# FFN token operands made between the first products, and an attention merge that advances three times per attention step

## The chip, the cores and the metric

The kernel runs on one core of one Trainium2 chip. The metric is the device time of one execution in microseconds (us); of several runs the median is taken.

## What is computed

Two layers of an encoder over 1024 tokens with 1024 channels. Each layer has three residual steps. The change touches the end of the first and the beginning of the second.

```
h = rms_norm(x);  z = h @ w_in
merged = concat(rms_norm(o_attn), rms_norm(o_gm), rms_norm(o_conv))   # windowed attention, spatial gating, conv
x = x + merged @ w_out                                                # the mixer
hf = rms_norm(x, norm_ffn_g) @ w_gate_up                              # 1024 x 5632
x = x + (silu(hf[:, :2816]) * hf[:, 2816:]) @ w_down                  # the FFN
x = x + (p @ w_ple_proj) * sigmoid(rms_norm(x) @ w_ple_gate)
```

## The kernel before

**Layout and products.** Channels lie on the 128 partitions, tokens along the free axis, in two halves of 512 tokens. Every product of fp32 numbers is made of three fp32r matmuls (`step_mm`, L220 to L229): high part by high part, high by low, low by high. The high part is a rounded copy (`copy_h`, L122, on ACT), the low part is the rest (`sub_l` L125, `scaled_l` L128, on DVE). `load_w` (L205 to L217) loads 512 KB of weights from the SP queue into one of 3 buffers `raw`, makes the high part `wh` (L122 on ACT, or L215 on the engine handed in) and the low part `wl` (L216, on DVE or POOL); `wh` and `wl` have 3 buffers each. 38 tiles of 128 x 1024 (`U`) serve nearly everything else. The PSUM banks are three `pa` (`BA`), four `pt` (`BT`) and one `po`.

**Order of the work.** Each engine executes its instructions in one fixed order. It comes from the order of the code, which a scheduler of the framework then moves within limits at build time, and from generators that the code advances by hand: `bg.tick()` is called within products and advances the background generators by their rates. The attention is one such generator, `att_gen` (L963). One of its steps, t, handles one block of 128 tokens of one group of heads in five parts that end in `yield`; after the eighth block of a half of the tokens it starts that half's `merge_attn` (L924), which multiplies by the softmax denominators (L942, L943), squares and sums over channels (L944 on ACT, L946 on POOL, L950 on PE), takes the power -0.5 (L270, POOL), spreads it over the partitions (L281, PE) and writes the operands `mhl` (L957, L122, L128). A merge has 10 parts, and `att_gen` advances it once per step (L1034), at the end of the step.

**Mixer's end.** `wo_first` multiplies the parts of `w_out` that need no attention. `bg.until(att, ...)` (L1255) then runs the attention until half 0 is merged. `wo_second(0)` (L1085) adds the attention part for half 0, takes the sum into X (L1100, DVE), makes the FFN operands `hl` of that half (`norm_add`) and the norm's factor per token, `nrm[0].bc` (`norm_stat` L292 and L270, `norm_bcast` L281 and L298; the tile is named `st`).

**FFN.** The gate and up products are made by a scheme with seven products in place of eight for each pair of 128 output columns, over two halves of the tokens and two of the channels. `first(j)` (L1119) makes the products of half 0 for pair j: 48 matmuls into four banks, which DVE takes out (L1138, L1140, L1141, L1145), and writes two partial results to memory from the ACT queue. `token_forms(k)` (L1160), for k = 0 to 3, makes the other token operands `tf`: four rows of X times gain and norm (`normed`, L1157, DVE), differences of them (L1167, L1169 on DVE, L1168, L1172 on POOL) and five splits into high and low (L122 ACT, L125 DVE). `load_rest(j)` (L1179) loads the pair's weights into four tiles `rw` and one `sm`, and `rest(j)` (L1191) forms sums of weights on POOL (L1228 to L1231), splits them (L122, L125) and makes 120 matmuls on `tf`. There are 11 pairs. The order is first(0) to first(3), the rest of the attention, first(4), `wo_second(1)`, the four `token_forms`, first(5) to first(7) (`BEHIND` = 3), and then rest(0), first(8), rest(1), first(9), rest(2), first(10), rest(3) to rest(10). While `ahead` is true (first(0) to first(4)) the weights' high parts are made on DVE and the low parts on POOL, and `first` uses the three `pa` banks alone; later it uses all seven.

Of the kernel before, what the change touches and what calls it, by code (L numbers as in the profile page):

```python
# [43 lines left out]
PLE_LAG = 2  # L44
NP2 = NF // 2
AHEAD = 4
BEHIND = 3

C1 = 1
C2 = 2.0  # L50
# [21 lines left out]
def tile_encoder_trunk(ctx: ExitStack, tc: tile.TileContext, x, p, positions, norm_mix_g, w_in,  # L72
# [389 lines left out]
    for layer in range(DEPTH):  # L462
# [461 lines left out]
        def merge_attn(hb):  # L924
# [27 lines left out]
            r = small(4, "ar")  # L952
            rsqrt_cols(r, ps[:, 0:4], 1.0 / 512)
            yield
            ps = bcast_rows(r)
            for kt, o in enumerate(os):
                nc.vector.tensor_tensor(out=o, in0=o, in1=ps, op=ALU.mult)  # L957
# [5 lines left out]
        def att_gen():  # L963
# [4 lines left out]

            def at(i):
                return items[i] if 0 <= i < n else None  # L970

            def aside():
                while side:
                    if next(side[0], bg) is bg:
                        side.pop(0)
                    else:
                        break

            yield from q_split(0, 0)
            for t in range(n + 3):  # L980
                while zqs[at(t + 1).kv if at(t + 1) else 0] is None:
                    yield
                x, y, z, w = at(t), at(t - 1), at(t - 2), at(t - 3)
                nx = at(t + 1)
                if nx and nx.b % 2 == 0:
                    side.insert(0, q_split(nx.kv, nx.b // 2))
                if x:
                    x.begin()
                if y:
                    y.peak()  # L990
                    y.exp(0)
                if x:
                    x.score(0)
                yield
                if w:
                    w.value(2)
                    w.out()
                    if (t - 3) % 8 == 7:
                        merging.append(merge_attn((t - 3) // 8))
                aside()  # L1000
                yield
                if y:
                    y.exp(1)
                if z:
                    z.turn(0)
                if x:
                    x.score(1)
                aside()
                yield
                if y:  # L1010
                    y.exp(2)
                if z:
                    z.turn(1)
                if x:
                    x.score(2)
                yield
                if z:
                    z.value(0)
                if y:
                    y.exp(3)  # L1020
                aside()
                yield
                if z:
                    z.turn(2)
                if x:
                    x.score(3)
                if z:
                    z.value(1)
                aside()
                yield  # L1030
                if nx and nx.b % 2 == 0:
                    while (nx.kv, nx.b // 2) not in qts:
                        aside()
                for g_ in list(merging):  # L1034
                    if next(g_, bg) is bg:
                        merging.remove(g_)
            for g_ in merging:
                yield from g_

# [79 lines left out]
        def first(j):  # L1119
# [1 line left out]
            hl0, bc = nrm[0].hl, nrm[0].bc  # L1121
            c0 = 2 * j * P
            ws = [load_w(rows_of(w_gate_up[layer], 0, NK, off + c0, P), (NK, P),
                         nc.gpsimd if ahead else None, nc.vector if ahead else None)
                  for off in (0, DFF)]
            a, sm = T("sg"), U("sm")
            for i, (wh, wl) in enumerate(ws):
# [31 lines left out]

        def token_forms(k):  # L1160

            for hf in range(2):
                for m in (k, k + HK):
                    normed(hf, m)
            b11, b21, b12, b22 = X[0][k], X[0][k + HK], X[1][k], X[1][k + HK]
            t1 = T("t1")
            nc.vector.tensor_tensor(out=t1, in0=b12, in1=b11, op=ALU.subtract)  # L1167
# [93 lines left out]
        first(AHEAD)  # L1261
        wo_second(1)
        ahead = False
        for k in range(HK):
            token_forms(k)
        for j in range(AHEAD + 1, AHEAD + 1 + BEHIND):
            first(j)
        for j in range(NP2):
            load_rest(j)
            rest(j)  # L1270
# [151 lines left out]
```

## Time and profile before

| what | value |
|---|---|
| runs | 2505.62, 2507.15 and 2503.2 us; median 2505.62 us |
| the profiled execution | 2507.3 us, its span 2505.5 us |
| TensorE (PE) busy | 2327.1 us, 93% of the span |
| VectorE (DVE) busy | 1493.4 us, 60% |
| ScalarE (ACT) busy | 915.8 us, 37% |
| GpSimd (POOL) busy | 730.1 us, 29% |
| mean granted TensorE clock | 0.967 of full speed |

The two layers do the same work: a place at t us in layer 0 is found again some 1235 us later in layer 1. In layer 0 the attention ends and `wo_second(0)` starts at about 365 us, `wo_second(1)` runs from 474.6 to 496.4 us, and rest(0) starts at 556 us. In the rows, "idle before" is the time in which an engine stood still before an instruction, and "<-" names what ended it. Bracketed numbers in a timeline are the same for one instruction.

### The profile page before, as it was taken

How to read it: one execution, taken by the hardware profiler on the slowest of the kernel's cores; microseconds unless marked ns; L12 is line 12 of the kernel's file. 1: busy time of each engine (PE TensorE's matmuls, PEld its weight loads, DVE VectorE, ACT ScalarE, POOL GpSimd, SP SyncE). 2: the span in 40 equal slices, each digit the busy share in tenths (PEclk: the TensorE clock that was granted, in tenths of full speed). 3: DMA queues.
4: the chain of work that ended last, by engine and by line, in shares of the span. 5: the costliest groups of instructions: out<-in, count | busy, mean ns of one | idle time of the engine just before them, and what ended most of it. 6: DMA issues, size and time to landing. Idle time of an engine off the chain costs nothing. (4 is left out here: it accounts for less than half of the span.)

```text
span 2505.5 us, 30172 instructions
## 1 busy us (share of the span) xinstructions
PE 2327.1 (93%) x11404; PEld 1950.1 (78%) x11404; DVE 1493.4 (60%) x2307; ACT 915.8 (37%) x1610; POOL 730.1 (29%) x529
## 2 busy tenths in 40 slices
PE   7997977969999999999999898879689999999999
PEld 6996766847788888888789876768577888888887
DVE  7996676475665553626469666755856555526252
ACT  4346572132232243424323455612322222425242
POOL 4122415541344300104321233255424342001031
PEclk9998998989999999999999999989899999999999
DMA  6110513632543245543321123135345341736332
GB/s 200 44 55 9 177 34 97 214 110 93 190 163 110 94 161 174 176 135 106 100 68 39 35 76 110 58 119 181 101 160 173 118 146 52 234 123 210 100 91 70
DMA packets 237010, 294.78 MB, mean 118 GB/s; under 512 B 10644, under 2 KB 180208, under 8 KB 236864
## 3 DMA queue, kind: packets, MB, share of 16 engines
q1 hardware_dynamic: 217696, 248.55, 30.9%
q10 hardware_dynamic: 18688, 44.06, 4.8%
q8 instruction: 90, 1.47, 0.2%
q0 software_dynamic: 480, 0.24, 0.1%
q14 instruction: 56, 0.46, 0.1%
HBM read 228.84 MB, written 63.96 MB: 117 GB/s over the span
## 5 line engine op out<-in xcount | busy, mean ns | idle before, releaser
L216 DVE TENSOR_TENSOR wl<-raw,wh 128x1024 fp32r<-128x1024 f32 x172 | 216.7, 1260 | 255.3 <-ACT wh L122 249.8
L122 ACT ACTIVATE wh<-raw 128x1024 fp32r<-128x1024 f32 x172 | 182.0, 1058 | 438.2 <-PE pt L226 302.5
L226 PE MATMUL pt<-tf,wh 128*128 128x512 f32 x792 | 308.2, 389 | 0.0
L224 PE MATMUL pt<-tf,wh 128*128 128x512 f32 x792 | 306.1, 390 | 0.0
L228 PE MATMUL pt<-tf,wl 128*128 128x512 f32 x792 | 304.6, 389 | 0.0
L224 PE MATMUL pa<-tf,wh 128*128 128x512 f32 x704 | 277.3, 396 | 23.5 <-ACT wh L122 23.5
L264 POOL TENSOR_TENSOR st<-st,sq 128x512 f32<-128x512 f32 x82 | 121.4, 1482 | 596.9 <-ACT sq L263 594.9
L226 PE MATMUL pa<-tf,wh 128*128 128x512 f32 x704 | 278.2, 395 | 0.0
L228 PE MATMUL pa<-tf,wl 128*128 128x512 f32 x704 | 273.4, 393 | 0.0
L224 PE MATMUL pa<-hl,wh 128*128 128x512 f32 x564 | 228.1, 406 | 16.4 <-DVE sg L1141 10.9
L226 PE MATMUL pa<-hl,wh 128*128 128x512 f32 x564 | 225.6, 400 | 2.9 <-DVE hl L128 2.7
L228 PE MATMUL pa<-hl,wl 128*128 128x512 f32 x564 | 223.9, 397 | 0.0
L1228 POOL TENSOR_TENSOR ws<-rw,rw 128x512 f32<-128x512 f32 x44 | 70.1, 1593 | 410.6 <-DMA rw<-in_w_gate_up_dram 214.6
L608 PE MATMUL pa<-wh,hl 128*128 128x256 f32 x640 | 179.9, 287 | 7.0 <-ACT zq L621 3.7
L610 PE MATMUL pa<-wl,hl 128*128 128x256 f32 x640 | 181.9, 286 | 0.2 <-DVE wl L216 0.2
L611 PE MATMUL pa<-wh,hl 128*128 128x256 f32 x640 | 180.9, 286 | 0.0
L224 PEld LDWEIGHTS pa<-tf,wh 128*128 128x128 f32 x704 | 134.7, 191 | 55.1 <-ACT wh L122 26.9
L228 PEld LDWEIGHTS pt<-tf,wl 128*128 128x128 f32 x792 | 148.7, 188 | 31.1
L224 PEld LDWEIGHTS pt<-tf,wh 128*128 128x128 f32 x792 | 148.7, 188 | 30.9
L226 PEld LDWEIGHTS pt<-tf,wh 128*128 128x128 f32 x792 | 148.7, 188 | 30.6
L125 DVE TENSOR_TENSOR wl<-rw,wh 128x512 fp32r<-128x512 f32 x176 | 140.8, 804 | 32.5 <-ACT wh L122 32.4
L228 PEld LDWEIGHTS pa<-tf,wl 128*128 128x128 f32 x704 | 134.2, 191 | 28.6
(320 smaller groups left out, 5029.6 us busy)
## 6 DMA issues: line engine op xcount, KB each, us to landing
rw<-in_w_gate_up_dram SPq DMA_DIRECT2D x88, 512.0 KB, 6.9
raw<-in_w_down_dram SPq DMA_DIRECT2D x88, 512.0 KB, 3.6
raw<-in_w_gate_up_dram SPq DMA_DIRECT2D x44, 512.0 KB, 4.4
ac<-act SPq DMA_DIRECT2D x88, 256.0 KB, 4.3
raw<-in_w_ple_gate_dram SPq DMA_DIRECT2D x32, 512.0 KB, 4.2
raw<-in_w_in_dram SPq DMA_DIRECT2D x28, 512.0 KB, 3.8
raw<-in_w_out_dram SPq DMA_DIRECT2D x24, 512.0 KB, 4.2
sum<-sm ACTq DMA_DIRECT2D x22, 512.0 KB, 5.3
```

The source lines that it names most:

```text
L122: nc.scalar.activation(dst, src, AF.Copy, scale=scale)
L125: nc.vector.tensor_tensor(out=dst, in0=src, in1=f(h), op=ALU.subtract)
L216: (eng or nc.vector).tensor_tensor(out=l, in0=raw, in1=f(h), op=ALU.subtract)
L224: nc.tensor.matmul(b, lhsT=wh, rhs=hl[:, 0:512], start=first, stop=False, skip_group_check=again)
L226: nc.tensor.matmul(b, lhsT=wh, rhs=hl[:, 512:1024], start=False, stop=False, skip_group_check=again)
L228: nc.tensor.matmul(b, lhsT=wl, rhs=hl[:, 0:512], start=False, stop=last, skip_group_check=again)
L264: (eng or nc.gpsimd).tensor_tensor(out=n.s, in0=n.s, in1=sq, op=ALU.add)
L608: nc.tensor.matmul(o, lhsT=x_[:, th], rhs=wh, start=(kc + k == 0), stop=False)
L610: nc.tensor.matmul(o, lhsT=x_[:, th], rhs=wl, start=False, stop=False)
L611: nc.tensor.matmul(o, lhsT=x_[:, tl], rhs=wh, start=False, stop=(kc == 1 and k == 3))
L1228: tt(out=s3, in0=a21, in1=a22, op=ALU.add)
```

## The change

Three things are changed. In the mixer, `merge_attn` has two more empty parts (12 in all before the end), and `att_gen` advances it at three places of each step instead of one, so that a merge ends some four steps after its half's last block, not ten; `bg.until` is satisfied earlier, and the last attention steps are then left to the ticks within `wo_second(0)` and the first products. In `first`, the high part of the up weights is made on ACT in the stage `ahead` (it was DVE), and the low part of the gate weights on POOL in the later stage (it was DVE). In the FFN, half 0 of X is no longer normalised in `token_forms` on DVE: for all eight rows ACT multiplies by the gain and POOL by the norm, in place; and `BEHIND` is 6, so that all 11 first products come before rest(0), with `token_forms(n)` written after first(5 + n).

```diff
--- before.py
+++ after.py
@@ -44,7 +44,7 @@
 PLE_LAG = 2
 NP2 = NF // 2
 AHEAD = 4
-BEHIND = 3
+BEHIND = 6
 
 C1 = 1
 C2 = 2.0
@@ -952,6 +952,8 @@
             r = small(4, "ar")
             rsqrt_cols(r, ps[:, 0:4], 1.0 / 512)
             yield
+            yield
+            yield
             ps = bcast_rows(r)
             for kt, o in enumerate(os):
                 nc.vector.tensor_tensor(out=o, in0=o, in1=ps, op=ALU.mult)
@@ -968,6 +970,11 @@
 
             def at(i):
                 return items[i] if 0 <= i < n else None
+
+            def merge_step():
+                for g_ in list(merging):
+                    if next(g_, bg) is bg:
+                        merging.remove(g_)
 
             def aside():
                 while side:
@@ -997,6 +1004,7 @@
                     w.out()
                     if (t - 3) % 8 == 7:
                         merging.append(merge_attn((t - 3) // 8))
+                merge_step()
                 aside()
                 yield
                 if y:
@@ -1013,6 +1021,7 @@
                     z.turn(1)
                 if x:
                     x.score(2)
+                merge_step()
                 yield
                 if z:
                     z.value(0)
@@ -1031,9 +1040,7 @@
                 if nx and nx.b % 2 == 0:
                     while (nx.kv, nx.b // 2) not in qts:
                         aside()
-                for g_ in list(merging):
-                    if next(g_, bg) is bg:
-                        merging.remove(g_)
+                merge_step()
             for g_ in merging:
                 yield from g_
 
@@ -1121,7 +1128,8 @@
             hl0, bc = nrm[0].hl, nrm[0].bc
             c0 = 2 * j * P
             ws = [load_w(rows_of(w_gate_up[layer], 0, NK, off + c0, P), (NK, P),
-                         nc.gpsimd if ahead else None, nc.vector if ahead else None)
+                         nc.gpsimd if ahead or off == 0 else None,
+                         nc.vector if ahead and off == 0 else None)
                   for off in (0, DFF)]
             a, sm = T("sg"), U("sm")
             for i, (wh, wl) in enumerate(ws):
@@ -1159,9 +1167,8 @@
 
         def token_forms(k):
 
-            for hf in range(2):
-                for m in (k, k + HK):
-                    normed(hf, m)
+            for m in (k, k + HK):
+                normed(1, m)
             b11, b21, b12, b22 = X[0][k], X[0][k + HK], X[1][k], X[1][k + HK]
             t1 = T("t1")
             nc.vector.tensor_tensor(out=t1, in0=b12, in1=b11, op=ALU.subtract)
@@ -1261,10 +1268,13 @@
         first(AHEAD)
         wo_second(1)
         ahead = False
-        for k in range(HK):
-            token_forms(k)
-        for j in range(AHEAD + 1, AHEAD + 1 + BEHIND):
-            first(j)
+        for m in range(NK):
+            copy_h(X[0][m], X[0][m], col("ffn", layer, m))
+            nc.gpsimd.tensor_tensor(out=X[0][m], in0=X[0][m], in1=nrm[0].bc, op=ALU.mult)
+        for n in range(BEHIND):
+            first(AHEAD + 1 + n)
+            if n < HK:
+                token_forms(n)
         for j in range(NP2):
             load_rest(j)
             rest(j)
```

In the tables of order below, a row is a source line, an operation, the tile written and those read. A tile's number tells one buffer use from another.

The first place is PE in layer 0 behind `wo_second(0)`, where half 1's merge meets first(0). Before, the merge's sum (L950) and spreading (L281) stand within first(0), in front of half 0's own sum (L292):

```order
L224 MATMUL pa_4062<-hl_3882,wh_4049 128x512
L226 MATMUL pa_4062<-hl_3882,wh_4049 128x512
L228 MATMUL pa_4062<-hl_3882,wl_4050 128x512
L950 MATMUL pt_3895<-ones,as_3803 128x1 x4
L281 MATMUL pt_3910<-ident,ar_3900 128x128 x4
L224 MATMUL pa_4062<-hl_3920,wh_4049 128x512
L292 MATMUL po_4033<-ones,st_2500 128x1 x4
```

Now L950 of half 1 stands within first(3) (`wh_4262`), and its L281 within first(4) (`wh_4353`), 25 matmuls later:

```order
L224 MATMUL pa_4326<-hl_3779,wh_4262 128x512
L226 MATMUL pa_4326<-hl_3779,wh_4262 128x512
L228 MATMUL pa_4326<-hl_3779,wl_4263 128x512
L950 MATMUL pt_4241<-ones,as_4164 128x1 x4
L224 MATMUL pa_4326<-hl_3812,wh_4262 128x512
L226 MATMUL pa_4326<-hl_3812,wh_4262 128x512
```

The two instructions have moved behind some three of the first products, and no matmul of first(0) stands behind them any more.

The second place is POOL at the same time in layer 0: the norm's power (`rcol`) and what follows it. Before:

```order
L264 TENSOR_TENSOR st_2500<-st_2500,sq_4029 128x512
L270 TENSOR_TENSOR rcol_4038<-ms_4039,mhalf 128x4
L216 TENSOR_TENSOR wl_4132<-raw_4130,wh_4131 128x1024
L216 TENSOR_TENSOR wl_4202<-raw_4200,wh_4201 128x1024
L216 TENSOR_TENSOR wl_4208<-raw_4206,wh_4207 128x1024
```

Now:

```order
L264 TENSOR_TENSOR st_2500<-st_2500,sq_3886 128x512
L216 TENSOR_TENSOR wl_4036<-raw_4034,wh_4035 128x1024
L270 TENSOR_TENSOR rcol_3895<-ms_3896,mhalf 128x4
L1273 TENSOR_TENSOR X_3576<-X_3576,st_2500 128x512 x2
L1273 TENSOR_TENSOR X_3577<-X_3577,st_2500 128x512 x2
L1273 TENSOR_TENSOR X_3578<-X_3578,st_2500 128x512 x2
L1273 TENSOR_TENSOR X_3579<-X_3579,st_2500 128x512 x2
L216 TENSOR_TENSOR wl_4139<-raw_4137,wh_4138 128x1024
```

A split of first(1)'s up weights has moved in front of the power, and the eight new multiplications stand directly behind it, in front of first(2)'s weights.

The third place is DVE in layer 0 after half 1's norm, where the banks of first(5) have to be emptied. Before, `L1138` for the first `pt` bank comes behind the 8 products L1157, the differences and nine splits; the last rows ahead of it:

```order
L1169 TENSOR_TENSOR X_3777<-X_4431,t_783_4689 128x512
L1140 TENSOR_TENSOR pt_4843<-pt_4843,st_2500 128x512
L125 TENSOR_TENSOR tf_4621<-X_3776,tf_4621 128x512
L125 TENSOR_TENSOR tf_4624<-X_4428,tf_4624 128x512
L125 TENSOR_TENSOR tf_4628<-t_765_4617,tf_4628 128x512
L125 TENSOR_TENSOR tf_4631<-X_3778,tf_4631 128x512
L125 TENSOR_TENSOR tf_4634<-X_4430,tf_4634 128x512
L125 TENSOR_TENSOR tf_4645<-X_3776,tf_4645 128x512
L125 TENSOR_TENSOR tf_4648<-X_4428,tf_4648 128x512
L125 TENSOR_TENSOR tf_4652<-t_771_4641,tf_4652 128x512
L125 TENSOR_TENSOR tf_4655<-X_3778,tf_4655 128x512
L1138 TENSOR_TENSOR sm_4722<-pt_4723,st_2500 128x512
```

Now the same step (L1146) stands directly behind half 1's eight products (now L1165), and the differences (L1174, L1176) alternate with the emptying of banks:

```order
L1165 SCALAR_TENSOR_TENSOR X_4429<-X_4429,cols_178,st_2501 128x512
L1165 SCALAR_TENSOR_TENSOR X_4431<-X_4431,cols_178,st_2501 128x512
L1146 TENSOR_TENSOR sm_4642<-pt_4643,st_2500 128x512
L216 TENSOR_TENSOR wl_4735<-raw_4733,wh_4734 128x1024
L1146 TENSOR_TENSOR sm_4642<-pt_4673,st_2500 128x512
L1149 TENSOR_TENSOR sg_4641<-pa_4657,sm_4642 128x512
L1174 TENSOR_TENSOR t_777_4707<-X_4428,X_3576 128x512
L1149 TENSOR_TENSOR pa_4687<-pa_4687,sm_4642 128x512
L216 TENSOR_TENSOR wl_4833<-raw_4831,wh_4832 128x1024
L1176 TENSOR_TENSOR X_3576<-X_4430,t_777_4707 128x512
L1153 TENSOR_TENSOR sg_4641<-pa_4687,sg_4641 128x512
L1148 TENSOR_TENSOR pt_4785<-pt_4785,st_2500 128x512
```

The operations that make token operands have moved from ahead of the first bank to between the banks.

## Rows read from the trace of the kernel before

**Rows 1.** The page's first lines: the span, and PE's busy time with its share of the span.

```profile
span 2505.5 us, 30172 instructions
PE 2327.1 (93%) x11404; PEld 1950.1 (78%) x11404; DVE 1493.4 (60%) x2307; ACT 915.8 (37%) x1610; POOL 730.1 (29%) x529
```

**Rows 2.** Busy time by stretch, layer 0. Columns: the stretch and its length, busy us (and instructions) of PE, PE's weight loads, DVE, ACT and POOL, then the granted TensorE clock, the DMA share and GB/s.

```profile
345.00:365.50 20.50, 16.42 (x98) 12.45 (x97) 15.75 (x47) 17.48 (x48) 4.18 (x6) 0.98 0.00 1
409.00:416.00 7.00, 7.00 (x21) 5.75 (x21) 6.06 (x10) 3.75 (x7) 1.59 (x2) 0.50 0.00 0
431.20:436.50 5.30, 5.30 (x13) 4.14 (x14) 1.99 (x4) 0.61 (x1) 1.24 (x1) 0.50 0.49 140
536.00:556.00 20.00, 15.79 (x60) 11.93 (x60) 17.92 (x28) 4.21 (x9) 10.57 (x8) 0.93 0.73 250
599.00:641.00 42.00, 39.97 (x168) 32.54 (x168) 25.50 (x33) 10.08 (x16) 11.37 (x9) 0.96 0.37 126
641.00:683.00 42.00, 40.03 (x169) 32.66 (x169) 25.62 (x34) 10.53 (x18) 12.24 (x9) 0.96 0.36 123
710.00:737.00 27.00, 27.00 (x120) 22.35 (x120) 14.62 (x24) 7.56 (x13) 11.07 (x8) 1.00 0.37 127
```

**Rows 3.** PE's longest waits from 350 to 480 us (layer 0): what waited, for what, us in total, times, the longest.

```profile
PE pa L224 <- DVE sg L1141: 5.3, 1, 5.3
PE pt L281 <- POOL ar L270: 4.7, 1, 4.7
PE pt L950 <- POOL as L946: 2.4, 1, 2.4
PE pa L224 <- ACT hl L122: 2.1, 1, 2.1
```

**Rows 4.** PE's timeline in layer 0, the instructions behind idle time (start us, us, operation, idle before and who ended it): the norm of half 1, first(5) to first(7), and the starts of rest(0) to rest(3).

```profile
505.91 0.65 PE L281 MATMUL pt<-ident,rcol 128*128 128x128 f32 x4 [0.30 <-POOL rcol L270]
535.88 0.76 PE L224 MATMUL pt<-hl,wh 128*128 128x512 f32 x1 [18.29 <-DVE sm L1138]
556.06 0.80 PE L224 MATMUL pa<-tf,wh 128*128 128x512 f32 x1 [3.94 <-ACT wh L122]
598.95 0.50 PE L224 MATMUL pa<-tf,wh 128*128 128x512 f32 x1 [2.97 <-ACT wh L122]
641.17 0.74 PE L224 MATMUL pa<-tf,wh 128*128 128x512 f32 x1 [2.21 <-ACT wh L122]
682.95 0.50 PE L224 MATMUL pa<-tf,wh 128*128 128x512 f32 x1 [1.80 <-ACT wh L122]
```

**Rows 5.** The same view in layer 1: half 1's merge, first(0), first(5) to first(7), and the starts of rest(1) to rest(3).

```profile
1634.60 1.87 PE L950 MATMUL pt<-ones,as 128*128 128x1 f32 x8 [2.37 <-POOL as L946]
1640.32 1.12 PE L281 MATMUL pt<-ident,ar 128*128 128x128 f32 x4 [3.85 <-POOL ar L270]
1643.58 0.79 PE L224 MATMUL pa<-hl,wh 128*128 128x512 f32 x1 [2.15 <-ACT hl L122]
1666.53 0.79 PE L224 MATMUL pa<-hl,wh 128*128 128x512 f32 x1 [5.30 <-DVE sg L1141]
1771.64 0.77 PE L224 MATMUL pt<-hl,wh 128*128 128x512 f32 x1 [18.62 <-DVE sm L1138]
1834.97 0.50 PE L224 MATMUL pa<-tf,wh 128*128 128x512 f32 x1 [4.17 <-ACT wh L122]
1877.11 0.50 PE L224 MATMUL pa<-tf,wh 128*128 128x512 f32 x1 [2.13 <-ACT wh L122]
1917.88 0.79 PE L224 MATMUL pa<-tf,wh 128*128 128x512 f32 x1 [2.37 <-ACT wh L122]
```

**Rows 6.** DVE's timeline in layer 0: the normalisation of X (half 0, then half 1) and the emptying of first(5)'s banks.

```profile
422.54 3.55 DVE L1157 SCALAR_TENSOR_TENSOR X<-X,cols,st 128x512 f32<-128x512 f32 x2
426.62 2.72 DVE L1157 SCALAR_TENSOR_TENSOR X<-X,cols,st 128x512 f32<-128x512 f32 x4
...
507.22 5.39 DVE L1157 SCALAR_TENSOR_TENSOR X<-X,cols,st 128x512 f32<-128x512 f32 x8 [0.87 <-ACT st L298]
...
520.75 0.69 DVE L1140 TENSOR_TENSOR pt<-pt,st 128x512 f32<-128x512 f32 x1
...
535.05 1.27 DVE L1138 TENSOR_TENSOR sm<-pt,st 128x512 f32<-128x512 f32 x2
```

**Rows 7.** Groups of instructions from 496 to 556 us (layer 0): line, engine, operation, tiles, count, busy us, mean ns of one, idle before.

```profile
L1168 POOL TENSOR_TENSOR X<-X,X 128x512 f32<-128x512 f32 x4 | 13.7, 3446 | 7.4 <-DVE t L1167 7.4
L122 ACT ACTIVATE tf<-X 128x512 fp32r<-128x512 f32 x16 | 8.9, 616 | 10.8 <-POOL X L1172 5.1 <-POOL X L1168 3.4 <-DVE X L1169 2.3
L1172 POOL TENSOR_TENSOR X<-X,X 128x512 f32<-128x512 f32 x4 | 5.8, 1487 | 0.0
L216 DVE TENSOR_TENSOR wl<-raw,wh 128x1024 fp32r<-128x1024 f32 x4 | 4.9, 1220 | 0.2 <-ACT wh L122 0.2
```

**Rows 8.** Groups over the whole span: a weight split on POOL, and a POOL operation on two SBUF tiles of 128 x 512 elsewhere in the kernel.

```profile
L216 POOL TENSOR_TENSOR wl<-raw,wh 128x1024 fp32r<-128x1024 f32 x44 | 110.5, 2513 | 60.9 <-DVE wh L215 53.8 <-PE pa L228 6.1
L1380 POOL TENSOR_TENSOR X<-sg,X 128x512 f32<-128x512 f32 x31 | 41.2, 1333 | 92.6 <-DVE sg L1373 92.6
```

**Rows 9.** POOL's timeline at half 1's norm in layer 0, and the page's DMA issues of the rests' weights (count, KB each, median us from issue to landing).

```profile
504.84 1.02 POOL L270 TENSOR_TENSOR rcol<-ms,mhalf 128x4 f32<-128x4 f32 x1 [4.99 <-DVE ms L268]
...
rw<-in_w_gate_up_dram SPq DMA_DIRECT2D x88, 512.0 KB, 6.9
```

## Prediction

> **What bounds the kernel now.** I read the page's engine totals first. PE is busy for 2327 of 2505.5 us; VectorE, next, for 60% [rows 1]. So the time is PE's work plus the places where PE stands still or runs at a lower clock, and this change adds and takes no matmul. All it can do is close such places or open new ones. The second view is therefore PE's waits and its timeline around the edited code, and the third the granted clock by stretch, because PE comes back slowly from a stop: from 409 to 416 us, behind a run of short waits, and from 431.2 to 436.5 us, behind one of 5.3 us, the granted clock is 0.50, the lower level of 1.2 GHz [rows 2]. A matmul then takes twice its time, so these stretches cost 3.5 and 2.65 us beside the waits themselves. While rests and firsts run undisturbed the clock is 1.00 and PE is busy for 27.00 of 27 us [rows 2].
>
> Three places of each layer stand out. First, half 1's attention merge beside first(0): waits of 2.4, 4.7, 2.1 and 5.3 us in layer 0 [rows 3], of 2.37, 3.85, 2.15 and 5.30 us in layer 1 [rows 5]. Second, the token forms: PE stops for 18.29 us ahead of first(5)'s last banks, released by DVE's L1138 [rows 4], and for 18.62 us in layer 1 [rows 5]. Third, the starts of rests with a first ahead of them: 2.97, 2.21 and 1.80 us for rest(1) to rest(3) [rows 4], 4.17, 2.13 and 2.37 us in layer 1 [rows 5], each released by ACT's cast.
>
> The sum below is made against the profiled execution's 2507.3 us; the median of the runs is 1.7 us lower.
>
> **Term 1: token forms between the firsts.** Why PE stops for 18 us is seen on DVE: it makes eight normalisations, the differences and nine splits before it empties first(5)'s banks at 535.05 [rows 6], and it waits in between for POOL, whose L1168 takes 3446 ns [rows 7]. In the changed order L1146 (before, L1138) stands right behind half 1's eight normalisations, and each later first has one quarter of the forms beside it. The wait goes, with about 1.4 us of clock behind it (0.07 of 20 us at a clock of 0.93 [rows 2]); for both layers 18.29 + 18.62 + 2.8 = 39.7 us.
>
> What is late next:
> - The norm's spreading (L281) waits 0.30 us for `rcol` [rows 4], since matmuls stand between the sum and it. Now none does, and POOL's power of 1.02 us [rows 9] with DVE's step ahead of it lies bare: +1.1 a layer.
> - Rest(0)'s weights are queued on SP behind more firsts' loads; a load lands 6.9 us after its issue [rows 9]. Bounds 0 and 5; I take +2, since there are three more firsts (32 us) to load in. On ACT the same three firsts bring their stores forward, two each; they are issued beside other firsts, and no cast of a rest stands behind them but rest(0)'s.
> - DVE nearly fills up in the four firsts that carry forms: 2 differences, 5 splits and 7 emptyings at 0.69 us [rows 6] and a weight split of 1.22 [rows 7] make 10.9 us, where 48 matmuls take PE 27.0/120 x 48 = 10.8 [rows 2]. Seven banks against four a first let PE run up to three quarters of a first, 8 us, ahead. Bounds 0 and 10; I take +3, the end that the slack is nearest to.
>
> The added 6.1 a layer leave 39.7 - 12.2 = **27.5 us**. Taking gate splits from DVE (1.22) to POOL (2.51 [rows 8]) is covered: POOL has 10.57 us of work in the 20 us from 536 [rows 2].
>
> **Term 2: all firsts before the rests.** A rest behind a rest starts without a wait; one behind a first waits, since its casts stand in ACT's order behind the first's DMA issues, which wait for the last emptying. Rest(1) to rest(3) lose that place: 2.97 + 2.21 + 1.80 = 6.98 and 4.17 + 2.13 + 2.37 = 8.67 us. Their stretches of 42 us run at 0.96 [rows 2] where 1.00 is granted undisturbed, so 1.7 us each in the four that hold a single first and rest, 6.8. Sum **22.4 us**, bounds 15 (the waits alone) and 24. Rest(0)'s wait of 3.94 [rows 4] stays.
>
> **Term 3: the merge, and half 0's normalisation off DVE.** Half 1's merge moves from first(0) to first(3) and first(4), where everything it needs is made a first or more before. Its waits of 2.4 and 4.7 us for POOL go. The 5.3 us [rows 3] end with DVE's L1141, and DVE is late there because six L1157 of half 0 (6.3 us from 422.54 on [rows 6]) stand in front of the banks; these go to ACT and POOL, so I count the wait out. With the one for `hl` and the clock: 14.5 + 3.5 + 2.65 = 20.6 us, and with layer 1's waits of 13.67, at the same clock, 19.8: 40.4 us.
>
> What takes their place: `rcol` of half 0 now stands on POOL behind a split (L216) of 2.51 us [rows 8] whose high part comes from ACT, and ACT now has eight in-place copies of 0.62 us (the nearest row, 616 ns [rows 7]) to fit in. I take 4 us for the wait of L281 and 2 for clock, +6 a layer (behind L281 on PE stand the last attention steps and the first products, behind `rcol` on POOL the L1273), so 40.4 - 12 = **28.4 us**. Two further costs have no row. The last attention steps run beside `wo_second(0)`; PE has 4.1 us idle in 345 to 365.5, where ACT is already busy for 17.48 of 20.5 us [rows 2]. Now more work on ACT (copies 4.9 us, casts of up weights) comes in behind it. At best the steps' idle time of up to 4 us a layer is filled by matmuls of `wo_second(0)`, and one or two other waits with it (+7 a layer); at worst ACT is late for `hl` by twice its added 4.9 us (-10 a layer). I take nothing, between the two, and keep 28.4 - 20 to 28.4 + 14, about 8 to 42, for the range. The eight L1273 on POOL, 8 x 1.33 to 1.49 = 10.7 to 11.9 us [rows 7, 8], stand ahead of first(2)'s weights. First(0) and first(1), 21.6 us of PE, cover them; without that cover first(2) would start up to 12 us late.
>
> **Sum.** 27.5 + 22.4 + 28.4 = 78.3 us, so 2507.3 - 78.3 = 2429.0 for such an execution, and less 1.7 **2428 us** for the median.
>
> **Rivals.**
>
> *A: DVE and POOL hold each other up beside first(5) to first(8).* For: L1168 takes 3446 ns while DVE runs operations with two SBUF inputs; the like operation L1172 takes 1487 ns right behind it [rows 7], and L1380 elsewhere 1333 [rows 8]. Against: in 536 to 556 us POOL's and DVE's shares add up to more than the stretch (10.57 + 17.92 of 20 us [rows 2]), since emptying a bank has one input in PSUM. If the two shut each other out, a form's SBUF operations on DVE (2 differences, 5 splits, one gate or up split: 6.0 us), POOL's (2 sums and a split, 2 x 1.4 + 2.5 = 5.3) and 7 emptyings of 4.8 would need 16 us in a first of 10.8: 5.3 x 4 = 21 us late a layer, of which the banks' 8 us of slack swallow a part. That is +13 a layer, 2454 us. It decides if POOL's operations there last over 3 us each.
> The Trainium skill ("SBUF — State Buffer", section "Who interferes with whom") says that a DVE instruction with two SBUF inputs and a GpSimd instruction that reads SBUF shut each other out, and that the one that started first keeps the ports for the whole instruction. The 3446 against 1487 ns of this trace agree in direction [rows 7]; by that rule this rival would be the forecast, 2454, not 2428.
>
> *B: the mixer's end gets crowded on ACT.* The wait moves from the merge to `hl` and the casts, and the gain of term 3 goes: 2428 + 28 = 2456. For: ACT's 17.48 of 20.5 us [rows 2] and the wait for `hl` that is there already [rows 3]. Against: in 536 to 556 ACT has only 4.21 us of work, and the copies may be done late.
>
> *C, slower: the rests starve for weights.* Before, a first stood ahead of three rests and gave their loads 10.8 us more; now eleven rests follow each other. If each of ten rests in a layer waited for a landing, 6.9 us [rows 9], that would be 138 us, 2428 + 138 = 2566. It turns into a loss from 78.3/20 = 3.9 us a rest on. Against: in 710 to 737 rests already follow each other and PE is busy for 27.00 of 27 us [rows 2].
>
> *D: the gaps only move.* PE's stops are filled, and DVE, at 11 us of work a first, gives back the same time in the firsts: 2505. For: DVE's busy 17.92 of 20 us [rows 2]; against: PE stops there for one block of 18 us, while DVE's work is the same sum over 65 us of PE.
>
> **How the numbers follow.** Forecast 0.66, A 0.15, B 0.12, C 0.04, D 0.03. A measurement of this kernel can tell about 0.2%, 5 us, from no change. Forecast, A and B are faster by more than that: 0.93; D is within it: 0.03; C is slower: 0.04. The predicted time is the forecast's, 2428. The range takes in A and B, and B with term 1's upper bounds in one layer (10 in place of 3, 5 in place of 2): up to 2456 + 10 = 2466. Downwards it takes term 3's upper bound, 14, and term 1's costs that are not paid, 12: 2402. Outside are C, D and the case of A and B together.
>
> **What would show it right or wrong.** Right: no PE wait near 18 us at first(5); one waiting rest start a layer, rest(0); no wait at the merge's sum and spreading; one of some 4 us at L281 behind `wo_second(0)`; the mean granted clock above 0.967. A would show as POOL operations of 3 us and more in first(5) to first(8) and PE waits for DVE's L1149 or L1153; B as PE waits for `hl` and `wh` of ACT from 350 to 420 us; C as waits of each rest for DMA. The prediction is wrong in its mechanism if the firsts with forms cost much more than 10.8 us each, or if the rests' starts still wait though no first stands ahead of them.

## The result and the profile after

The changed kernel takes 2420.21 us (median of 4 runs, 2419.41 to 2421.81), the kernel before, beside it, 2506.39. The ratio is 0.9658, 95% interval 0.9642 to 0.9675: 86 us faster, where 78 were forecast (2428, range 2402 to 2466).

The first lines of the page after, against [rows 1]:

```profile
span 2418.1 us, 30182 instructions
PE 2306.6 (95%) x11404; PEld 1940.1 (80%) x11404; DVE 1463.0 (61%) x2269; ACT 937.5 (39%) x1636; POOL 755.2 (31%) x557
```

The number of PE's instructions is the same. Its busy time is 20.5 us less, which goes with the granted clock (0.979 on average, before 0.967); the other 67 us of 87 were idle time. PE's longest waits after, from 340 to 745 us (what waited, for what, us in total, times, longest):

```profile
PE pa L224 <- ACT wh L122: 6.8, 1, 6.8
PE pt L281 <- POOL rcol L270: 3.8, 2, 2.5
PE pa L224 <- DVE sm L1146: 2.5, 2, 2.1
PE pa L224 <- DVE X L1107: 1.9, 1, 1.9
```

The 18.3 us at first(5) [rows 4] and the merge's 2.4, 4.7 and 2.1 us [rows 3] are gone. Of the rests' waits, four with 10.9 us in layer 0 [rows 4], one is left, longer than any before: rest(0)'s 6.8 us. Busy time by stretch, in the columns of [rows 2]:

```profile
345.00:365.50 20.50, 20.50 (x106) 17.41 (x106) 16.96 (x36) 17.75 (x40) 7.18 (x6) 1.00 0.42 140
380.00:400.00 20.00, 14.25 (x61) 11.46 (x60) 11.21 (x19) 11.33 (x23) 13.90 (x10) 0.83 0.41 125
520.00:540.00 20.00, 18.73 (x80) 14.58 (x79) 19.90 (x26) 9.65 (x15) 8.47 (x5) 1.00 0.39 142
540.00:560.00 20.00, 13.18 (x50) 10.39 (x49) 15.92 (x20) 4.20 (x7) 9.93 (x8) 0.83 0.97 334
```

From 345 to 365.5 us, where PE had 4.1 us idle in the last attention steps, it no longer pauses; but other work stands there now, since `wo_second(0)` starts at 342 us and not at about 365 (PE's timeline after):

```profile
342.05 0.96 PE L224 MATMUL pa<-mhl,wh 128*128 128x512 f32 x3 [0.51 <-ACT mhl L122]
```

From 520 to 540 us, in the firsts with token forms, DVE is busy for 19.90 of 20 us. From 540 to 560 us PE waits for rest(0)'s weights and then runs slowly.

**Where the time went, by place.** Three marks lie at the same point of the work in both kernels: half 1's norm (L281), rest(0)'s first matmul, and the rests' last. Groups of matmuls on `tf`: count, shortest/median/longest ns, first and last start; in each kernel layer 0, then layer 1. Before:

```profile
L224 PE MATMUL pa<-tf,wh x352: 389/389/796, 556.1 to 1140.0; 128*128 128x512 f32 x176
L224 PE MATMUL pt<-tf,wh x396: 387/389/478, 571.3 to 1142.7; 128*128 128x512 f32 x198
...
L224 PE MATMUL pa<-tf,wh x352: 387/389/793, 1790.8 to 2376.4; 128*128 128x512 f32 x176
L224 PE MATMUL pt<-tf,wh x396: 388/389/486, 1806.2 to 2379.2; 128*128 128x512 f32 x198
```

After:

```profile
L224 PE MATMUL pa<-tf,wh x352: 389/389/795, 553.8 to 1094.4; 128*128 128x512 f32 x176
L224 PE MATMUL pt<-tf,wh x396: 387/389/481, 569.5 to 1097.1; 128*128 128x512 f32 x198
...
L224 PE MATMUL pa<-tf,wh x352: 387/389/792, 1748.7 to 2289.1; 128*128 128x512 f32 x176
L224 PE MATMUL pt<-tf,wh x396: 387/389/481, 1764.3 to 2291.9; 128*128 128x512 f32 x198
```

The norm's mark stands at 505.9 before [rows 4] and at 1741.4 in layer 1 (first line). After (PE's timeline, both layers; the other lines):

```profile
1741.35 0.65 PE L281 MATMUL pt<-ident,rcol 128*128 128x128 f32 x4 [0.30 <-POOL rcol L270]
...
394.46 1.12 PE L281 MATMUL pt<-ident,rcol 128*128 128x128 f32 x4 [2.46 <-POOL rcol L270]
485.46 0.65 PE L281 MATMUL pt<-ident,rcol 128*128 128x128 f32 x4 [1.35 <-POOL rcol L270]
553.81 0.80 PE L224 MATMUL pa<-tf,wh 128*128 128x512 f32 x1 [6.82 <-ACT wh L122]
...
1678.96 0.65 PE L281 MATMUL pt<-ident,rcol 128*128 128x128 f32 x4 [1.35 <-POOL rcol L270]
1748.69 0.79 PE L224 MATMUL pa<-tf,wh 128*128 128x512 f32 x1 [5.42 <-ACT wh L122]
```

Three firsts (32.4 us of PE) have moved from behind rest(0)'s start to ahead of it, so they are added to the second stretch of before and taken from the third:

| stretch | layer 0, before - after | layer 1 | gain | forecast |
|---|---|---|---|---|
| to half 1's norm (term 3) | 505.9 - 485.5 = 20.4 | 598.7 - 581.9 = 16.8 | 37.2 | 28.4 |
| norm to rest(0) (term 1) | 82.6 - 68.3 = 14.3 | 81.8 - 69.7 = 12.1 | 26.4 | 27.5 |
| rest(0) to the rests' end (term 2) | 554.2 - 543.3 = 10.9 | 556.0 - 543.2 = 12.8 | 23.7 | 22.4 |

They make 87.3 of the spans' 87.4 us. Terms 1 and 2 look exact; the experiments below show what stands behind that.

The first stretch, both layers together, as the sum of 0 to 505.9 and 1142.7 to 1741.4 us before, of 0 to 485.5 and 1097.1 to 1679.0 us after (length, then each engine's busy us):

```profile
sum 1104.60, PE 994.45 PEld 853.55 DVE 739.63 ACT 476.42 POOL 388.49; mean PE 497.22 PEld 426.78 DVE 369.82 ACT 238.21 POOL 194.24
sum 1067.40, PE 980.42 PEld 846.98 DVE 735.87 ACT 498.42 POOL 416.55; mean PE 490.21 PEld 423.49 DVE 367.93 ACT 249.21 POOL 208.28
```

So 23.2 of its 37.2 us are idle time of PE, and 14.0 are busy time.

### The profile page after: what moved, and what is told of

Its sections match the earlier page's. It is cut to its first block, busy times and chain, and to the rows that moved or that the text cites. A ratio compares the mean times of both kernels' runs of the same rounds, so it can differ in the third digit from the quotient of the medians.

```text
span 2418.1 us, 30182 instructions
## 1 busy us (share of the span) xinstructions
PE 2306.6 (95%) x11404; PEld 1940.1 (80%) x11404; DVE 1463.0 (61%) x2269; ACT 937.5 (39%) x1636; POOL 755.2 (31%) x557
## 5 line engine op out<-in xcount | busy, mean ns | idle before, releaser
L216 DVE TENSOR_TENSOR wl<-raw,wh 128x1024 fp32r<-128x1024 f32 x160 | 203.2, 1270 | 255.8 <-ACT wh L122 249.8
L122 ACT ACTIVATE wh<-raw 128x1024 fp32r<-128x1024 f32 x182 | 192.4, 1058 | 400.9 <-PE pt L226 241.5
L224 PE MATMUL pa<-tf,wh 128*128 128x512 f32 x704 | 274.5, 392 | 12.2 <-ACT wh L122 12.2
L226 PE MATMUL pa<-tf,wh 128*128 128x512 f32 x704 | 275.4, 391 | 0.0
L216 POOL TENSOR_TENSOR wl<-raw,wh 128x1024 fp32r<-128x1024 f32 x56 | 138.7, 2478 | 74.6 <-ACT wh L122 58.7
L122 ACT ACTIVATE wh<-rw 128x512 fp32r<-128x512 f32 x176 | 105.6, 623 | 143.2 <-PE pt L226 71.1
```

The costliest lines, as they stand in the source:

```text
L122: nc.scalar.activation(dst, src, AF.Copy, scale=scale)
L216: (eng or nc.vector).tensor_tensor(out=l, in0=raw, in1=f(h), op=ALU.subtract)
L224: nc.tensor.matmul(b, lhsT=wh, rhs=hl[:, 0:512], start=first, stop=False, skip_group_check=again)
L226: nc.tensor.matmul(b, lhsT=wh, rhs=hl[:, 512:1024], start=False, stop=False, skip_group_check=again)
```

## Experiments

Times are medians; "before" stands for the runs of the kernel before beside them (2503.01 us in the first four, 2505.47 and 2504.94 in the next two fours, 2506.39 beside the changed kernel, so a difference from the changed kernel is good to some 3 us). Line numbers are each run's own: the step L1138 of the kernel before is L1146 in the changed kernel and L1145 in some runs.

**merge_alone**: the kernel before with the two added `yield`s and the three `merge_step()` of the change's diff, nothing else.

> The kernel before with the merge's edit alone (three advances a step, two empty parts). Theory: the mixer's gain (37.3 us of the 87 between the two traces) comes mostly from the merge: half 1's waits in first(0) go (2.4 + 4.7 + 2.1 and 2.37 + 3.85 + 2.15 = 17.6 us) with the low clock behind them (3.5 a layer), and the attention's 4.1 us of idle time a layer; first(0)'s wait of 5.3 us for DVE stays, or most of it. About -25 to -32 us: 2475 to 2481. Rival (half 0's normalisation, taken off DVE, carries the gain): -10 us or less, 2496 or more.

Measured 2463.83 us, ratio 0.9847 (0.9826 to 0.9868), -39 us. More than expected, and it takes away L1141's wait of 5.3 us too: of the long stops in first(0) to first(3) none is left (one of 2.48 us comes later), though half 0 is still normalised on DVE (PE's timeline):

```profile
387.20 1.02 PE L292 MATMUL po<-ones,st 128*128 128x1 f32 x8 [1.69 <-DVE ro L922]
391.71 1.11 PE L281 MATMUL pt<-ident,rcol 128*128 128x128 f32 x4 [3.49 <-POOL rcol L270]
448.96 0.50 PE L224 MATMUL pa<-hl,wh 128*128 128x512 f32 x1 [2.48 <-DVE sm L1145]
```

**norm_alone**: the kernel before with half 0's normalisation on ACT and POOL alone.

```diff
-            for hf in range(2):
-                for m in (k, k + HK):
-                    normed(hf, m)
+            for m in (k, k + HK):
+                normed(1, m)
 ...
+        for m in range(NK):
+            copy_h(X[0][m], X[0][m], col("ffn", layer, m))
+            nc.gpsimd.tensor_tensor(out=X[0][m], in0=X[0][m], in1=nrm[0].bc, op=ALU.mult)
```

> The kernel before with half 0's normalisation on ACT and POOL alone. Theory: first(0)'s wait of 5.3 us for DVE goes with 2.65 us of low clock, in both layers: -12 to -16 us, 2490 to 2494; the wait of 18 us at the token forms stays, since half 0's eight rows were normalised 85 us ahead of it. Rival (it carries the mixer's gain): -25 us or more. Second rival (the 5.3 us wait is the merge's, not the normalisation's): within 4 us of before.

2497.53 us, ratio 0.9976 (0.9963 to 0.9989): -5.5 us, less than expected and just outside the second rival's 4. The 5.3 us shrink to 1.57, but behind them PE waits anew, for the weight split that POOL makes behind the eight products:

```profile
431.89 0.50 PE L224 MATMUL pa<-hl,wh 128*128 128x512 f32 x1 [1.57 <-DVE sg L1141]
433.99 0.80 PE L228 MATMUL pa<-hl,wl 128*128 128x512 f32 x1 [1.36 <-POOL wl L216]
```

**late_rests_alone**: the kernel before with `BEHIND = 6`.

> The kernel before with all eleven firsts ahead of rest(0), token forms where they were. Theory: the starts of rest(1) to rest(3) stop waiting, with the clock behind them: -20 to -24 us, 2482 to 2486; the 18 us at the token forms stay. Rival (the wait for weights collects at rest(0)): half of it or less, -12 us or less, with a wait at rest(0) of 8 us and more.

2466.83 us, ratio 0.9859 (0.9838 to 0.9879): -36 us, more than expected, and not by the rival: rest(0)'s own wait (3.94 us before [rows 4]) is down to 1.29, with the 18 us still there:

```profile
533.03 0.76 PE L224 MATMUL pt<-hl,wh 128*128 128x512 f32 x1 [18.29 <-DVE sm L1138]
583.68 0.50 PE L228 MATMUL pa<-tf,wl 128*128 128x512 f32 x1 [1.29 <-DVE wl L125]
```

By the marks of the table, 24.7 of the 40.4 us between the two traces lie behind rest(0)'s start, as expected, and 8.0 between half 1's norm and rest(0). The other 7.7 lie ahead of half 1's norm, where the edit changes nothing; they stay open.

**forms_ahead**: the changed kernel with its forms ahead of first(5).

```diff
+        for k in range(HK):
+            token_forms(k)
         for n in range(BEHIND):
             first(AHEAD + 1 + n)
-            if n < HK:
-                token_forms(n)
```

> The changed kernel with its four token forms ahead of first(5) again, everything else as changed. Theory: the term measured between the traces comes back, +24 to +30 us, 2444 to 2450, as one PE wait of 12 to 18 us a layer for L1146. Rival of the shared SBUF ports: POOL's sums in the forms, 1.3 us in the changed kernel, last 2.5 us and more where DVE's operations with two SBUF inputs stand back to back, as 3.4 us before; if POOL was only slow for another reason they stay at 1.3 to 1.5 us.

2436.64 us, ratio 0.9738 (0.9718 to 0.9758): +16 us against the changed kernel (20 by the two ratios), not 24 to 30. The PE wait is back with 17.51 us, but rest(0) no longer waits 6.8 (1.30). So in layer 0 putting the forms between the firsts buys back 17 us and pays 5.5 us of them at rest(0); from half 1's norm to rest(0), forms_ahead takes 11.1 and 9.6 us more than the changed kernel. POOL's timeline beside the forms (start, us, operation, idle before):

```profile
497.17 4.95 POOL L216 TENSOR_TENSOR wl<-raw,wh 128x1024 fp32r<-128x1024 f32 x1 [8.80 <-ACT wh L122]
502.07 7.25 POOL L1175 TENSOR_TENSOR X<-X,X 128x512 f32<-128x512 f32 x4
509.29 6.73 POOL L1179 TENSOR_TENSOR X<-X,X 128x512 f32<-128x512 f32 x4
```

A sum takes 1.7 to 1.8 us (the changed kernel 1.3 to 1.4) and the split 4.95 in place of 2.4: longer beside dense DVE work, though not the 2.5 us and more of that rival. Why the sum L1168 took 3446 ns before [rows 7], with the forms in the same place, stays open.

**norm_back**: the changed kernel with norm_alone's edit undone.

> The changed kernel with half 0 normalised on DVE again (eight products), everything else as changed. After merge_alone, which lost the 5.3 us wait for L1141 too, my theory has fallen that half 0's normalisation on DVE caused it. New theory: the wait needs the two together, the merge's own DVE work in first(0) and the normalisation; with the merge gone from first(0), DVE has room, so this costs little: +0 to +4 us, 2420 to 2424. Rival (the first theory): +16 us, 2436, with PE waits of some 5 us for L1149 in first(0) to first(2).

2418.28 us, ratio 0.9654 (0.9637 to 0.9671), as the changed kernel within the intervals. Half 0's normalisation on DVE cost nothing once the merge was out of first(0).

**split_back**: the changed kernel with both edits in `load_w`'s call undone.

```diff
-                         nc.gpsimd if ahead or off == 0 else None,
-                         nc.vector if ahead and off == 0 else None)
+                         nc.gpsimd if ahead else None, nc.vector if ahead else None)
```

> The changed kernel with the weights' splits on the engines of before (up high parts on DVE in the first stage, gate low parts on DVE in the later firsts). Theory: DVE is the next engine in firsts that carry token forms (19.9 of 20 us busy), so 1.22 us more a first in four firsts a layer shows: +3 to +10 us, 2423 to 2430, as PE waits for DVE's L1146, L1153 or for splits, and a later rest(0). Rival (the seven banks' slack takes it): within 2 us of 2420.

2402.18 us, ratio 0.9588 (0.9573 to 0.9603): 18 us faster than the changed kernel, where both theories said slower or the same. DVE's groups from 488 to 548 us (count, busy us, mean ns, idle before), the changed kernel:

```profile
L1174 DVE TENSOR_TENSOR t<-X,X 128x512 f32<-128x512 f32 x4 | 7.4, 1843 | 0.0
L216 DVE TENSOR_TENSOR wl<-raw,wh 128x1024 fp32r<-128x1024 f32 x5 | 6.8, 1354 | 0.0
L125 DVE TENSOR_TENSOR tf<-t,tf 128x512 fp32r<-128x512 f32 x4 | 4.9, 1227 | 0.0
L1176 DVE TENSOR_TENSOR X<-X,t 128x512 f32<-128x512 f32 x4 | 4.6, 1161 | 0.0
```

and split_back:

```profile
L216 DVE TENSOR_TENSOR wl<-raw,wh 128x1024 fp32r<-128x1024 f32 x9 | 12.1, 1348 | 0.0
L1175 DVE TENSOR_TENSOR X<-X,t 128x512 f32<-128x512 f32 x4 | 3.6, 890 | 0.0
L1173 DVE TENSOR_TENSOR t<-X,X 128x512 f32<-128x512 f32 x4 | 2.7, 676 | 0.0
L125 DVE TENSOR_TENSOR tf<-t,tf 128x512 fp32r<-128x512 f32 x4 | 2.7, 676 | 0.0
```

The same difference (L1174, now L1173) takes 1843 ns on average where POOL makes splits, and 676 where it makes none. Single operations of the changed kernel show how (DVE's timeline, then POOL's):

```profile
495.00 2.12 DVE L1174 TENSOR_TENSOR t<-X,X 128x512 f32<-128x512 f32 x1
515.29 2.88 DVE L125 TENSOR_TENSOR tf<-t,tf 128x512 fp32r<-128x512 f32 x1
520.50 0.67 DVE L1174 TENSOR_TENSOR t<-X,X 128x512 f32<-128x512 f32 x1
...
494.17 2.41 POOL L216 TENSOR_TENSOR wl<-raw,wh 128x1024 fp32r<-128x1024 f32 x1 [8.76 <-ACT wh L122]
515.22 2.40 POOL L216 TENSOR_TENSOR wl<-raw,wh 128x1024 fp32r<-128x1024 f32 x1 [3.40 <-ACT wh L122]
```

Three of the four L1174 (2.12 to 2.29 us) and one of the four L125 of `t` (2.88) begin while a split runs on POOL, and each ends 0.54 or 0.55 us behind the split's end. The fourth L1174, with nothing on POOL beside it, takes 0.67. Four splits come back to DVE for 5.3 us, and 4.7 + 2.2 + 1.0 = 7.9 us of stretching goes.

**rw_ahead**: the changed kernel with each form ahead of its first, and rest(0)'s loads behind the last form.

```diff
         for n in range(BEHIND):
-            first(AHEAD + 1 + n)
             if n < HK:
                 token_forms(n)
+            first(AHEAD + 1 + n)
+            if n == HK - 1:
+                load_rest(0)
         for j in range(NP2):
-            load_rest(j)
+            if j:
+                load_rest(j)
```

> The changed kernel with each token form written ahead of its first instead of behind, and rest(0)'s loads written behind the last form, so that on SP they stand ahead of the three w_down loads. Theory: rest(0)'s wait of 6.82 and 5.42 us is late loads: the third w_down load stands 11.4 us on SP for a buffer that first(10)'s split frees, and the rw loads stand behind it. They go, with the low clock behind them: -12 to -18 us, 2402 to 2408. Rival (the rw loads have no tile before the forms are done, or PE waits for POOL's sums): rest(0) still waits 4 us and more, within 5 us of 2420. Second rival (forms ahead of the banks bring DVE waits into first(5) to first(8)): slower than 2420.

2420.31 us, ratio 0.9661: nothing. Rest(0) shows no wait, with its loads ahead of those for `w_down`; but from half 1's norm to rest(0) it takes 72.4 us in place of 68.3, since more comes back as DVE waits in the firsts:

```profile
505.43 0.56 PE L224 MATMUL pt<-hl,wh 128*128 128x512 f32 x1 [4.67 <-DVE sm L1146]
526.77 0.50 PE L228 MATMUL pt<-hl,wl 128*128 128x512 f32 x1 [2.22 <-DVE wl L216]
542.82 0.50 PE L228 MATMUL pt<-hl,wl 128*128 128x512 f32 x1 [2.14 <-DVE wl L216]
```

DVE was busy for 19.9 of 20 us in this stretch of the changed kernel, and here the order only chose where PE pays. The run moves forms and loads together, so what the loads' place is worth by itself is not shown.

**cast_later**: the changed kernel with `norm_bcast(nrm[0])` behind the first 12 matmuls of first(0).

> The changed kernel with the norm of half 0 spread over the partitions (L281) after the first 12 matmuls of first(0), not directly behind the sum. Theory: the new wait of 2.46 us for POOL's power and part of the low clock behind it (0.83 in the 20 us around it) go: -4 to -8 us, 2412 to 2416. Rival (PE has nothing ready there, since first(0)'s weights come as late): the wait turns up as one for wh or wl, within 2 us of 2420.

2419.81 us, ratio 0.9658, as the changed kernel. On PE, L281 moved only behind two matmuls of the attention (L906, L907), past none of first(0)'s; its wait fell from 2.46 to 1.50 us, while the sum's own wait ahead of it rose from 1.08 to 2.77. The edit didn't do what it was to do, so this tells nothing of the rival.

**gate_back**: the changed kernel with only the gate weights' low part back on DVE.

```diff
-                         nc.gpsimd if ahead or off == 0 else None,
+                         nc.gpsimd if ahead else None,
```

> The changed kernel with only the gate weights' low part back on DVE in the later firsts; the up weights' high part stays on ACT in the first stage. split_back gained 18 us where my theory said a loss. New theory: a split on POOL (2.4 to 2.9 us) holds up DVE's operations with two SBUF inputs (L1174 1843 ns with it, 676 without; L125 of t 1227 against 676): 8 us a layer lost against 5 us saved, and the late DVE holds back rest(0). Then the gate part carries the gain in the later firsts, where split_back stood 6 us a layer better, and some 12 of the 18 us come: 2406 to 2410. Rival (the up weights' casts on ACT in the first stage carry it): within 4 us of 2420.

2406.98 us, ratio 0.9606 (0.9592 to 0.9620): 13 of the 18 us, as the new theory had it. The other 5 go with the up weights' casts on ACT in the first stage. PE's wait of 2.1 us for DVE's L1146 at 453 us, which is still there in this run and not in split_back, does not carry them: splits_and_norm_back has one of 2.49 us there and is as fast as split_back. Which wait carries them stays open. From half 1's norm to rest(0) it is 6.0 and 6.3 us shorter than the changed kernel. DVE's own balance is only 7.9 - 5.3 = 2.6 us a layer; the rest lies in what follows it (rest(0)'s wait, 4.02 for 6.82 us, and the clock behind it), and was not taken apart.

**splits_and_norm_back**: split_back and norm_back together.

> The changed kernel with the splits and half 0's normalisation both as before, so that merge, forms between firsts and late rests are all that is left of the change. Theory: each was worth nothing or a loss (split_back -18, norm_back -2 us against the changed kernel), and they stand in different stages, so they add: 2398 to 2402. Rival (DVE, with both, is late in the first stage as before): 2406 or more, with PE waits for L1149 in first(0) to first(2).

2402.87 us, ratio 0.9591 (0.9575 to 0.9607): as split_back. Merge, forms between firsts and late rests alone are worth 102 us.

**sums_on_dve**: split_back with the forms' two sums on DVE.

```diff
-            nc.gpsimd.tensor_tensor(out=b12, in0=b22, in1=b12, op=ALU.subtract)
+            nc.vector.tensor_tensor(out=b12, in0=b22, in1=b12, op=ALU.subtract)
 ...
-            nc.gpsimd.tensor_tensor(out=b21, in0=b21, in1=b11, op=ALU.subtract)
+            nc.vector.tensor_tensor(out=b21, in0=b21, in1=b11, op=ALU.subtract)
```

> split_back with the token forms' two sums on DVE too (0.68 us each there, 8 a layer), so that POOL reads no SBUF beside first(5) to first(8). Theory of the shared ports: DVE's other operations fall to 0.68 and 1.21 us throughout, giving back some 2.5 us a layer of the 5.4 us that the sums add; net +2 to +8 us, 2404 to 2410. Rival (DVE's long operations have another cause, as DMA traffic): they stay at 1.3 us and more in places, and the time rises by 11 us or more.

2408.93 us, ratio 0.9614 (0.9600 to 0.9628), +7 us against split_back. Without POOL work beside them all of DVE's kinds are short (488 to 548 us):

```profile
L216 DVE TENSOR_TENSOR wl<-raw,wh 128x1024 fp32r<-128x1024 f32 x9 | 11.0, 1222 | 0.0
L125 DVE TENSOR_TENSOR tf<-X,tf 128x512 fp32r<-128x512 f32 x16 | 10.4, 696 | 0.0
L1175 DVE TENSOR_TENSOR X<-X,t 128x512 f32<-128x512 f32 x4 | 2.8, 692 | 0.0
```

So POOL's operations, not DMA traffic, stretched them. POOL was still the better place for the sums: 5.5 us of DVE work a layer saved, some 3 stretched.

**ahead_3**: splits_and_norm_back with `AHEAD = 3`, `BEHIND = 7`.

> splits_and_norm_back with three firsts before the rest of the attention in place of four, so that seven stand behind half 1's norm. Theory: the six firsts there are DVE's (some 68 us of its work to 65 of PE), so rest(0)'s last 4 us of wait are DVE's lack of time, and one more first without forms (7.3 us of DVE to 10.8 of PE) takes them away: -5 to -8 us a layer there; against it the merge's sum and its spreading (L950, L281) stand next to each other on PE again, +4 to +5 us a layer. Within 6 us of splits_and_norm_back. If rest(0) still waits 4 us, its wait is not DVE's.

2411.08 us, ratio 0.9621, 8 us slower than splits_and_norm_back: outside the 6. PE gets a wait of 4.50 us for DVE's L1145 where the merge meets first(3), and rest(0) still waits 4.55 us. From half 1's norm to rest(0) it takes 73.5 us with seven firsts, where splits_and_norm_back takes 62.3 with six, so the added first of 10.8 us brought nothing there. By what was written ahead, those last 4 us are then not DVE's lack of time; what they are stays open.

## Why the prediction was right, step by step

The signs that the prediction named came: no wait near 18 us at first(5), one waiting rest start, none at the merge's sum and spreading, 2.46 us at L281, a clock of 0.979. Its three terms hold to different degrees.

**Term 3 was under-sized** (28.4; 37.2 between the traces), and its cause was partly wrong. The merge's waits went as counted. But norm_back and merge_alone refute the sentence that six L1157 of half 0 make DVE late for L1141, if it is read as a need to take them off DVE: the merge's move alone removes that wait. They are a part of it, since without them 1.57 us are left in norm_alone. The merge alone brings 45.5 us of this stretch between the traces (483.1 and 576.0 us for 505.9 and 598.7; 39 by the medians), so the other edits in the mixer added nothing and took some back.

The missing 8.8 us are 3.0 of idle time (23.2 for the 28.2 - 8 = 20.2 of the sum) and 5.7 of busy time, which goes with the clock (14.0 for 12.3 - 4 = 8.3). The idle time has gains and losses that the sum leaves out: the attention's pauses, where "I take nothing" stands, and new waits of 1.9 us for L1107 and 2.1 us for L1146. A finer division is not shown, because traces of the same mixer code differ: this stretch takes 1061.9 us over both layers in rw_ahead, 1067.4 in the changed kernel. With ACT busy for 17.75 of 20.5 us, PE waits neither for `hl` nor for `wh` from ACT there, so rival B's waits didn't come; the up weights' casts on ACT still go with some 5 us (gate_back).

The +6 a layer for L281 was near: 2.46 us of wait (4 taken), and behind it a granted clock of 0.57 for 4 us, at most 1.7 us (2 taken). As much clock was lost ahead of it, behind the new wait of 1.86 us for L1107 (the columns of [rows 2]):

```profile
384.00:388.00 4.00, 4.00 (x11) 3.19 (x12) 1.89 (x4) 3.79 (x11) 2.87 (x3) 0.58 0.79 226
394.00:398.00 4.00, 3.54 (x19) 3.54 (x20) 1.76 (x3) 1.82 (x4) 2.13 (x3) 0.57 0.44 131
```

**Term 1 came out right** (27.5; 26.4) **by luck: two wrong sizes cancel.** "Taking gate splits from DVE to POOL is covered" is the step that failed: it counted POOL's free time and not what its operations do to DVE's. In gate_back the same stretch, from half 1's norm to rest(0), takes 62.3 and 63.4 us, so it gains 82.6 - 62.3 + 81.8 - 63.4 = 38.7 us against before, close to the 39.7 that I counted gross. The 12.2 us that I took off for DVE, rest(0) and the norm were thus hardly paid without the moved splits (rest(0) waits 4.02 us there, as before), and the 12.3 us that the splits cost, where I took nothing, stood in their place.

**Term 2** (22.4; 23.7) was right in size, but "rest(0)'s wait stays" was not: 3.94 us became 6.82 (5.42 in layer 1). Alone, the edit frees rest(0) instead (1.29) and gives 36 us. With the forms between the firsts the wait returns: three loads for `w_down` take 11.38 us on SP ahead of rest(0)'s loads, nearly all of it for a buffer that DVE frees with first(10)'s split. In rw_ahead, with rest(0)'s loads ahead of them, that wait is gone. SP's queue after:

```profile
529.17 11.38 SPq L211 DMA_DIRECT2D raw<-in_w_down_dram  x3
540.61 0.98 SPq L1191 DMA_DIRECT2D rw<-in_w_gate_up_dram  x2
```

**Rival A** had the right resource and the wrong victim. Its sign, POOL operations of 3 us and more, is absent (1.38 us for L1175, 2.6 for a split); it is DVE's operations that took three to four times as long where they met POOL's split (2.12 to 2.88 us for 0.68). Its other sign, PE waits for L1149 or L1153, came once in layer 0 (0.94 us); in layer 1 PE waits for DVE's splits instead (0.90 and 2.37 us). The Trainium skill ("SBUF — State Buffer", section "Who interferes with whom") says that whichever starts first keeps the shared ports for a whole instruction, so either engine can be the one that waits. This case agrees with both: POOL's 3446 ns before [rows 7], and after, DVE's operations that end just behind the split that began first. The 26 us that the rival priced came to 13 for the splits.

**C and D** didn't come as priced: rests behind rests do not wait, and gaps move only in part, to rest(0) in the changed kernel and within the firsts in rw_ahead.

## What to carry to other kernels

An operation that moves to an idle engine can slow the engine that it leaves: look at the duration of the same operations with and without it beside them. Where a chain of small steps (a merge, a norm) stands in front of a dense product, starting it some products earlier was worth 39 us here, and taking eight operations off DVE beside it 5.5. In the stretch where the second engine had no time left, changing the order only moved the wait (rw_ahead).

## What was not expected of the hardware

A DVE operation of two SBUF tiles, 676 ns alone, took 2.12 to 2.88 us where it began beside a POOL split of 2.4 to 2.9 us, which reads SBUF, and ended 0.54 or 0.55 us behind it; operations that empty a PSUM bank stayed at 0.68 us in the same stretch (L1146, 678 ns). POOL's split in turn took 4.95 us beside dense DVE work, 2.40 us elsewhere. Short stops of PE went with a low granted clock: 0.58 from 384 to 388 us behind stops of 0.34 and 1.86 us, 0.57 from 394 to 398 us behind stops of 1.08 and 2.46 us.
